# Modulation sums as four 256-column quarters on TensorE's column groups, and the state-space set-up spread over the weight units, in a two-layer hybrid encoder

## Chip, cores and metric

The kernel runs on one core of one Trainium2 chip. The metric is the device time of one execution in microseconds; several executions are timed and their median counts. The profile shows one execution, with its own time.

## What is computed

Two layers of a streaming encoder over 256 tokens of 1024 values, in fp32. Each layer is a SwiGLU feed-forward, a mixer of three heads (sparse attention, a state-space model, a convolution), and a second feed-forward. Each of the three is conditioned by a vector `c`: nine modulation rows of 1024 values per layer, `cond @ mod_w`, give shift, scale and gate.

```python
cond = silu(c)
for l in range(2):
    mod = cond @ mod_w[l] + mod_b[l]          # mod_w[l]: 1024 x 9216
    sh1, sc1, g1, sh2, sc2, g2, sh3, sc3, g3 = split(mod, 9)
    h = rms_norm(x, ffn1_norm[l]) * (1 + sc1) + sh1
    x = x + 0.5 * g1 * swiglu_ffn(h, ffn1_w_gu[l], ffn1_w_down[l])
    h = rms_norm(x, mix_norm[l]) * (1 + sc2) + sh2
    x = x + g2 * hybrid_mixer(h, ...)         # attention | state space | convolution
    h = rms_norm(x, ffn2_norm[l]) * (1 + sc3) + sh3
    x = x + 0.5 * g3 * swiglu_ffn(h, ffn2_w_gu[l], ffn2_w_down[l])
out = rms_norm(x, final_norm)
```

The state-space head needs matrices made from its parameters alone: powers of a complex step, and from them `W`, `O`, `R`, `Ec`, `Es` and `Tp`. The kernel calls this the set-up (`ssm_small`, `ssm_layer`). It doesn't depend on `x`, and must be done before the layer's mixer.

## The kernel before

**The weight stream.** All weights come as units of 128 x 1024 fp32 (`raw`, 512 KB, six buffers), loaded on SP's queue. A weight unit is split in two rounded parts, `hi` on ScalarE (line 100) and `lo` on VectorE (line 102), six buffers each, and each product is three matmuls (lines 328 to 330: hi by high part, lo by high part, hi by low part). A feed-forward works through 11 tiles of 256 hidden columns: four units of gate and up weights (`gt`, results `ps_gt`), then SiLU on ScalarE and the product `h` on VectorE (line 742), split as `hTh` and `hTl`, and then two units of down weights (`ps_y`) of the tile before. The two `ps_gt` banks are free for the next tile only when `h` has been made. In layer 0 the first three tiles run in `start` as `ps_gs`, together with the first modulation columns; their `h` is transposed (`ps_hT`).

**The modulation stream.** Between the weight units stand units of `mod_w` (plan: six of the nine rows in each first feed-forward, two or three in the second one of layer 0, one in the last). VectorE multiplies each by `cond` and adds it to a sum `macc` of 128 x 512 (line 365, two instructions per unit, eight for each half row; two sum buffers). When both halves of a row are there, `mod_flush` adds them over the partitions on TensorE (two fp32 matmuls with `ones`, line 389, to `ps_mod`), copies the result out on ScalarE (`mrow`, line 391), and writes it to DRAM with two transfers on POOL's queue (`spill`, line 394), from where it comes back as columns (`mcol`) or as a row for all partitions.

**The set-up** is a generator that yields after each small step. `stages` is called once for each weight unit (a tick) and takes steps from it: `SLOTS0` for layer 0 in its first feed-forward and `SLOTS1` for layer 1 in the second feed-forward of layer 0, each as first tick, number of ticks, steps per tick. In `start`, `SSTART` steps follow each of eight weight columns.

**The order.** A scheduler writes each engine's list of instructions from the program, its priorities and its own idea of durations. Each engine runs its list in order.

Of the kernel before, what the change touches and what calls it, by code (L numbers as in the profile page):

```python
# [13 lines left out]
AF = mybir.ActivationFunctionType  # L14
# [3 lines left out]
P = 128  # L18
# [8 lines left out]
ADG = (((0,),(1,),(2,3)),((0,1,2,3),))  # L27
HIP = 150
HIPT = 50
SLOTS0 = (4, 40, 2)  # L30
SSTART = 4
SLOTS1 = (2, 60, 2)
UW = 264
NEG_INADM = -3.0e38
NEG_TAKEN = -3.3e38
# [96 lines left out]
def kernel(  # L132
# [8 lines left out]
    nc = tc.nc  # L141
# [22 lines left out]
    def s2(shape, nm, tg="a", dtype=F32):  # L164
        return two_p.tile(shape, dtype, tag="s2" + tg, name=nm, bufs=S2B[tg])
# [15 lines left out]
    ones = const.tile([P, 32], F32, name="ones")  # L181
# [201 lines left out]
    def mod_flush():  # L383
        while len(finished) >= 2:
            l, m, _, acc0 = finished.pop(0)
            acc1 = finished.pop(0)[3]
            ps = bank(ps_m, "ps_mod")
            for h, acc in enumerate((acc0, acc1)):
                nc.tensor.matmul(ps[32 * h:32 * h + 32, :], ones, acc, start=True, stop=True, tile_position=(0, 32 * h))  # L389
            r = s2([64, 512], "mrow")  # L390
            nc.scalar.activation(r, ps[0:64, :], AF.Copy, scale=0.5 if m in (2, 8) else 1.0)  # L391
            d = spill[(l, m)] = tc.dram_tile([1, D], F32, name=f"spill{l}_{m}")
            for h in range(2):
                nc.gpsimd.dma_start(d[:, 512 * h:512 * h + 512], r[32 * h:32 * h + 1, :])  # L394
            if m % 3 != 2:
                nc.gpsimd.dma_start(mc(l, m), d[0].rearrange("(k p) -> p k", p=P))
            if m % 3 == 1:
                nc.gpsimd.tensor_scalar_add(mc(l, m), mc(l, m), 1.0)
                n0 = 8 * (L * (m // 3) + l)
                nc.gpsimd.tensor_mul(mc(l, m), mc(l, m), ncol[:, n0:n0 + 8])  # L400
# [418 lines left out]
    NL = G  # L819
    ssm = {}  # L820

    def ssm_small(l):
        e = nc.vector

        def cp(o, i, scale=1.0):
            nc.scalar.activation(o, i, AF.Copy, scale=scale)
# [3 lines left out]
        def B(nm, shape):  # L830
            n = math.prod(shape)
            if not pool8 or pool8[-1][1] + n > 2048:
                pool8.append([b8([P, 2048], "sp_tmp"), 0])
            t_, o_ = pool8[-1]
            pool8[-1][1] += n
            v_ = t_[:, o_:o_ + n]
            return v_ if len(shape) == 1 else v_.rearrange("p (d n) -> p d n", d=shape[0])
# [92 lines left out]
        yield  # L930

        PQr, PQi = B("pqr", [8, NL]), B("pqi", [8, NL])
        u8, v8 = B("u8", [8, NL]), B("v8", [8, NL])
        qrb = qr.rearrange("p (o n) -> p o n", o=1).to_broadcast([P, 8, NL])
        qib = qi.rearrange("p (o n) -> p o n", o=1).to_broadcast([P, 8, NL])
        cmul(PQr, PQi, PWr[:, 0:8, :], PWi[:, 0:8, :], qrb, qib, u8, v8)
        yield

        cA, cB = T("cA", [8, NL]), T("cB", [8, NL])
        lo_, hi_ = slice(0, 64), slice(64, 128)  # L940
        for tau in range(8):
            d_ = 7 - tau
            cp(cA[lo_, tau, :], PQr[lo_, d_, :])
            cp(cA[hi_, tau, :], PQi[hi_, d_, :])
            cp(cB[lo_, tau, :], PQi[lo_, d_, :], -1.0)
            cp(cB[hi_, tau, :], PQr[hi_, d_, :])
            if tau % 2:
                yield
        oA, oB = T("oA", [8, NL]), T("oB", [8, NL])
        cp(oA[lo_], PWr[lo_, 1:9, :])  # L950
        cp(oA[hi_], PWi[hi_, 1:9, :], -1.0)
# [538 lines left out]
        for g_ in gens:  # L1490
            yield from g_

    def stages(gen, first, n, per):

        def hook(u):
            if first <= u < first + n:
                for _ in range(per):
                    next(gen, None)
            elif u >= first + n:
                for _ in gen:  # L1500
                    pass
        return hook
# [74 lines left out]
```

## Time and profile before

| | |
|---|---|
| median of 3 runs | 1168.14 us (1165.55 to 1171.28) |
| the profiled execution, its own time | 1179.52 us |
| its span | 1177.7 us |
| TensorE busy | 1104.6 us, 94% of the span |
| VectorE busy | 880.2 us, 75% |
| ScalarE busy | 574.4 us, 49% |
| POOL busy | 78.3 us, 7% |
| mean granted clock of TensorE | 0.947 of full |

Busy time is that in which an engine worked on something; where it is near 100%, the engine's own work is the time. A matmul's record is longer than its share of the engine, since matmuls follow each other in a pipeline, so their price is read from one start to the next. The start lasts to about 88 us, the first feed-forward of layer 0 to about 262 us, its mixer to 405 us, its second feed-forward to 630 us; the first feed-forward of layer 1 ends at about 826 us, its mixer at 962 us.

### The profile page before, as it was taken

The page shows a single profiled execution, that of the slowest core. Times are in us where ns is not written, and L with a number is a line of the kernel's source. Part 1 is how long each engine was busy: PE and PEld are TensorE (multiplying, and loading weights), DVE is VectorE, ACT ScalarE, POOL GpSimd, SP SyncE. Part 2 cuts the span into 40 slices and gives each one's busy share as a digit, 9 for nine tenths or more (in the row PEclk, how much of TensorE's full clock was granted, in tenths as well). Part 3 has the DMA queues.
Part 4 walks back from the last instruction along what each step waited for, and adds up shares of the span by engine and source line. Part 5 has one row for each costly group of instructions (what it writes and reads, how often), then busy time and mean ns, then how long its engine had stood idle before and what let it go on. Part 6 is the DMA issues. An engine that isn't in the chain of part 4 may idle for free.

```text
span 1177.7 us, 19146 instructions
## 1 busy us (share of the span) xinstructions
PE 1104.6 (94%) x6979; PEld 944.4 (80%) x6979; DVE 880.2 (75%) x1763; ACT 574.4 (49%) x1035; POOL 78.3 (7%) x144
## 2 busy tenths in 40 slices
PE   5959999998989999889998999999899998999996
PEld 3549888877876779788986888888698687999986
DVE  4779888887667888887757888887667677665655
ACT  4484434346427565744445444443553656544442
POOL 5000021000021000001000000100000000000000
PEclk9979989999798999989999999999989699999999
DMA  9957999995452268678773999989355224767651
GB/s 249 295 182 248 310 312 319 325 282 148 122 118 87 90 197 293 207 229 259 226 223 93 331 337 347 321 300 291 101 157 128 90 89 136 246 209 217 212 162 54
DMA packets 181647, 251.44 MB, mean 214 GB/s; under 512 B 18998, under 2 KB 131840, under 8 KB 181552
## 3 DMA queue, kind: packets, MB, share of 16 engines
q1 hardware_dynamic: 173728, 240.56, 63.7%
q0 software_dynamic: 4768, 7.52, 2.9%
q10 hardware_dynamic: 3056, 2.13, 0.8%
q8 instruction: 55, 0.90, 0.3%
q14 instruction: 40, 0.33, 0.1%
HBM read 245.19 MB, written 1.11 MB: 209 GB/s over the span
## 4 chain that ended last, share of the span: by engine, by line
PE 78%; DVE 9%; DMA 7%; ACT 4%; issue 2%; POOL 0%; ACTq 0%; DVEq 0%; SPq 0%; POOLq 0%
PE ps_gt L328 11%; PE ps_gt L330 11%; PE ps_gt L329 11%; PE ps_y L329 7%; PE ps_y L330 7%; PE ps_y L328 7%; DMA raw<-in_mod_w_dram 3%; DVE lo L102 3%; PE ps_mod L389 2%; DMA U<-uT 1%; PE ps_idx L1198 1%; ACT hf L321 1%; PE ps_cv L1404 1%; PE ps_o L1267 1%; PE ps_gu L328 1%
## 5 line engine op out<-in xcount | busy, mean ns | idle before, releaser
L102 DVE TENSOR_TENSOR lo<-raw,hi 128x1024 fp32r<-128x1024 f32 (+1 forms) x314 | 378.6, 1212 | 141.1 <-ACT hi L100 138.4
L100 ACT ACTIVATE hi<-raw 128x1024 fp32r<-128x1024 f32 (+1 forms) x314 | 327.9, 1055 | 298.7 <-PE ps_gt L329 111.8
L328 PE MATMUL ps_gt<-xTh,hi 128*128 128x256 f32 x1120 | 320.6, 288 | 7.1 <-DVE h L742 7.1
L329 PE MATMUL ps_gt<-xTl,hi 128*128 128x256 f32 x1120 | 319.4, 286 | 0.0
L330 PE MATMUL ps_gt<-xTh,lo 128*128 128x256 f32 x1120 | 317.7, 287 | 0.0
L328 PEld LDWEIGHTS ps_gt<-xTh,hi 128*128 128x128 f32 x1120 | 218.0, 195 | 19.3 <-DVE h L742 7.4
L330 PEld LDWEIGHTS ps_gt<-xTh,lo 128*128 128x128 f32 x1120 | 216.9, 195 | 6.7 <-issue 5.9
L329 PEld LDWEIGHTS ps_gt<-xTl,hi 128*128 128x128 f32 x1120 | 218.6, 195 | 1.8 <-issue 0.8
L365 DVE SCALAR_TENSOR_TENSOR macc<-raw,cond,macc 128x512 f32<-128x512 f32 x224 | 166.4, 747 | 26.1 <-DMA raw<-in_mod_w_dram 24.1
L329 PE MATMUL ps_y<-lo,hTh 128*128 128x512 f32 x352 | 139.5, 396 | 0.9 <-DVE lo L102 0.9
L330 PE MATMUL ps_y<-hi,hTl 128*128 128x512 f32 x352 | 138.2, 393 | 1.0 <-DVE hTl L746 1.0
L328 PE MATMUL ps_y<-hi,hTh 128*128 128x512 f32 x352 | 136.9, 394 | 1.3 <-ACT hTh L745 1.2
L329 PEld LDWEIGHTS ps_y<-lo,hTh 128*128 128x128 f32 x352 | 66.8, 190 | 17.3 <-issue 2.5
L330 PEld LDWEIGHTS ps_y<-hi,hTl 128*128 128x128 f32 x352 | 66.8, 190 | 16.1 <-DVE hTl L746 2.1
L328 PEld LDWEIGHTS ps_y<-hi,hTh 128*128 128x128 f32 x352 | 66.6, 189 | 16.1 <-ACT hTh L745 2.6
L394 POOL DMA_DIRECT2D spill<-mrow x32 | 16.1, 508 | 716.1 <-ACT mrow L391 673.1
L740 ACT ACTIVATE silu<-ps_gt 128x256 f32<-128x256 f32 x70 | 25.7, 381 | 57.8 <-PE ps_gt L330 57.6
L742 DVE TENSOR_TENSOR h<-silu,ps_gt 128x256 f32<-128x256 f32 x70 | 28.5, 415 | 23.3 <-ACT silu L740 23.3
L328 PE MATMUL ps_gu<-hi,xTh 128*128 128x512 f32 x96 | 38.5, 402 | 5.9 <-DVE xTh L324 5.9
L330 PE MATMUL ps_gu<-hi,xTl 128*128 128x512 f32 x96 | 38.5, 401 | 3.1 <-DVE xTl L325 3.0
L329 PE MATMUL ps_gu<-lo,xTh 128*128 128x512 f32 x96 | 37.6, 392 | 0.0
L321 ACT ACTIVATE hf<-ps_ada,mcol 128x128 f32<-128x128 f32 x80 | 29.7, 471 | 10.6 <-PE ps_ada L316 8.6
(384 smaller groups left out, 1630.3 us busy)
## 6 DMA issues: line engine op xcount, KB each, us to landing
raw<-in_ffn_w_gu_dram SPq DMA_DIRECT2D x140, 512.0 KB
raw<-in_mod_w_dram SPq DMA_DIRECT2D x128, 512.0 KB
raw<-in_ffn_w_down_dram SPq DMA_DIRECT2D x88, 512.0 KB
raw<-in_ffn_w_gu_dram SPq DMA_DIRECT2D x72, 256.0 KB
raw<-in_w_in_dram SPq DMA_DIRECT2D x20, 512.0 KB
raw<-in_mod_w_dram SPq DMA_DIRECT2D x32, 256.0 KB
raw<-in_w_out_dram SPq DMA_DIRECT2D x16, 512.0 KB
row<-spill POOLq DMA_DIRECT2D x6, 512.0 KB, 3.9
```

The costliest lines, as they stand in the source:

```text
L100: nc.scalar.activation(hi[:, :n], raw[:, :n], AF.Copy)
L102: nc.vector.tensor_sub(lo[:, :n], raw[:, :n], hi[:, :n].bitcast(F32))
L321: hold[t]["hf", h] = nc.scalar.activation(hf[:, k, :], ps[:, P * k:P * k + P], AF.Identity, bias=mc(l, 3 * i)[:, kk:kk + 1], scale=mc(l, 3 ...
L328: return [nc.tensor.matmul(ps, xh, wh, start=start, stop=False), nc.tensor.matmul(ps, xh, wl, start=False, stop=False), nc.tensor.matmul(p ...
L329: nc.tensor.matmul(ps, xh, wl, start=False, stop=False),
L330: nc.tensor.matmul(ps, xl, wh, start=False, stop=stop)]
L365: nc.vector.scalar_tensor_tensor(acc, raw[:, 512 * i:512 * i + 512], cond[:, k:k + 1], prev, op0=ALU.mult, op1=ALU.add)
L389: nc.tensor.matmul(ps[32 * h:32 * h + 32, :], ones, acc, start=True, stop=True, tile_position=(0, 32 * h))
L394: nc.gpsimd.dma_start(d[:, 512 * h:512 * h + 512], r[32 * h:32 * h + 1, :])
L740: nc.scalar.activation(s, ps[i][:, :256], AF.Silu)
L742: nc.vector.tensor_mul(h, s, ps[i][:, 256:])
L1198: nc.tensor.matmul(ps[:, nk * i:nk * i + nk], qiT[32 * b:32 * b + 32, 256 * i + P * t:256 * i + P * t + P], kiT[32 * b:32 * b + 32, :nk], ...
```

## The change

The two sums of 512 columns become four of 256 columns, on all four column groups of TensorE, with an order token that keeps them together; the copy takes 128 x 256 for 64 x 512, and there are four spill transfers for two. The third number of `SLOTS0` and `SLOTS1` now is the number of steps, spread evenly over the ticks; `SSTART` is 2. In the set-up, the eight powers times `q` are made by doubling (three products of 1, 2 and 4 powers) in the order in which `cA` and `cB` need them, so that four copies on ScalarE do for 32. This makes the set-up one step shorter.

```diff
-SLOTS0 = (4, 40, 2)
-SSTART = 4
-SLOTS1 = (2, 60, 2)
+SLOTS0 = (1, 37, 43)
+SSTART = 2
+SLOTS1 = (1, 42, 58)
...
             ps = bank(ps_m, "ps_mod")
-            for h, acc in enumerate((acc0, acc1)):
-                nc.tensor.matmul(ps[32 * h:32 * h + 32, :], ones, acc, start=True, stop=True, tile_position=(0, 32 * h))
-            r = s2([64, 512], "mrow")
-            nc.scalar.activation(r, ps[0:64, :], AF.Copy, scale=0.5 if m in (2, 8) else 1.0)
+
+            for q in (3, 2, 1, 0):
+                mm_ = nc.tensor.matmul(ps[32 * q:32 * q + 32, 0:256], ones, (acc0, acc1)[q // 2][:, 256 * (q % 2):256 * (q % 2) + 256],
+                                       start=True, stop=True, tile_position=(0, 32 * q))
+                tc.stamp_issue_order_token(mm_.ins, f"mod{l}_{m}")
+            r = s2([P, 512], "mrow")
+            nc.scalar.activation(r[:, 0:256], ps[:, 0:256], AF.Copy, scale=0.5 if m in (2, 8) else 1.0)
             d = spill[(l, m)] = tc.dram_tile([1, D], F32, name=f"spill{l}_{m}")
-            for h in range(2):
-                nc.gpsimd.dma_start(d[:, 512 * h:512 * h + 512], r[32 * h:32 * h + 1, :])
+            for q in range(4):
+                nc.gpsimd.dma_start(d[:, 256 * q:256 * q + 256], r[32 * q:32 * q + 1, 0:256])
...
-        cmul(PQr, PQi, PWr[:, 0:8, :], PWi[:, 0:8, :], qrb, qib, u8, v8)
-        yield
+        e.tensor_copy(PQr[:, 7, :], qr)
+        e.tensor_copy(PQi[:, 7, :], qi)
+        for n in (1, 2, 4):
+            s_, d_ = slice(8 - n, 8), slice(8 - 2 * n, 8 - n)
+            cmul(PQr[:, d_, :], PQi[:, d_, :], PQr[:, s_, :], PQi[:, s_, :],
+                 PWr[:, n:n + 1, :].to_broadcast([P, n, NL]), PWi[:, n:n + 1, :].to_broadcast([P, n, NL]),
+                 t1[:, :n, :], t2[:, :n, :])
+            yield
...
-        for tau in range(8):
-            d_ = 7 - tau
-            cp(cA[lo_, tau, :], PQr[lo_, d_, :])
-            cp(cA[hi_, tau, :], PQi[hi_, d_, :])
-            cp(cB[lo_, tau, :], PQi[lo_, d_, :], -1.0)
-            cp(cB[hi_, tau, :], PQr[hi_, d_, :])
-            if tau % 2:
-                yield
+        cp(cA[lo_], PQr[lo_])
+        cp(cA[hi_], PQi[hi_])
+        cp(cB[lo_], PQi[lo_], -1.0)
+        cp(cB[hi_], PQr[hi_])
+        yield
...
-    def stages(gen, first, n, per):
+    def stages(gen, first, n, steps):
...
-                for _ in range(per):
+                i = u - first
+                for _ in range((i + 1) * steps // n - i * steps // n):
                     next(gen, None)
```

**How it moves the instructions.** On TensorE, the first modulation row in the first feed-forward of layer 0, before; its two matmuls stand in two places, the first behind a down unit and the second in the gate tile after it:

```order
L328 MATMUL ps_y_1046<-hi,hTh 128x512
L329 MATMUL ps_y_1046<-lo,hTh 128x512
L330 MATMUL ps_y_1046<-hi,hTl 128x512
L389 MATMUL ps_mod<-macc,ones 32x512
L328 MATMUL ps_gt_1203<-xTh,hi 128x256
...
L330 MATMUL ps_gt_1203<-xTh,lo 128x256
L389 MATMUL ps_mod<-macc,ones 32x512
L328 MATMUL ps_gt_1204<-xTh,hi 128x256
```

The same row after the change, in the gate tile that follows the start's three (line 390 is the new matmul's, line 994 a transpose of the set-up):

```order
L328 MATMUL ps_gt_1152<-xTh,hi 128x256
L329 MATMUL ps_gt_1152<-xTl,hi 128x256
L330 MATMUL ps_gt_1152<-xTh,lo 128x256
L390 MATMUL ps_mod<-macc,ones 32x256 x4
L994 MATMUL ps_cT<-ident,crr 128x128 x4
L328 MATMUL ps_gt_1153<-xTh,hi 128x256
```

The four stand together. The 32 matmuls of all sums stood in 29 places (26 alone and three pairs); the 64 of now stand in 16.

On VectorE, the end of the start, before: the first products of `W` and `O` (lines 1011 and 1013), then `lo` with the sums of `W` (line 1015) between, then the first `h` (line 756):

```order
L1011 TENSOR_TENSOR sl_O<-CRI,sp_oA 128x512 x4
L1031 TENSOR_TENSOR et<-sl_Ec 128x16
L102 TENSOR_TENSOR lo<-raw,hi 128x1024
L1032 TENSOR_TENSOR et<-sl_Es 128x16
L1015 TENSOR_TENSOR W<-W,wtmp 128x512
L102 TENSOR_TENSOR lo<-raw,hi 128x1024
...
L1015 TENSOR_TENSOR W<-W,wtmp 128x512
L102 TENSOR_TENSOR lo<-raw,hi 128x1024 x2
L1033 TENSOR_TENSOR sl_Ec<-et 128x16
L1013 TENSOR_TENSOR wtmp<-CRI,sp_oB 128x512
L756 TENSOR_TENSOR h<-silu,ps_gs_216 128x256
```

The same place after the change (the lines have moved down by 3; `sp_tmp` and `sp_m` are small set-up vectors):

```order
L102 TENSOR_TENSOR lo<-raw,hi 128x1024 x2
L894 TENSOR_TENSOR sp_tmp<-sp_er,sp_ei 128x16
L895 TENSOR_TENSOR sp_tmp<-sp_ei,sp_er 128x16
L914 TENSOR_TENSOR sp_m_671<-sp_m_671 128x16
L922 RECIPROCAL sp_tmp<-sp_tmp 128x16
L925 TENSOR_TENSOR sp_tmp<-sp_tmp 128x16
L102 TENSOR_TENSOR lo<-raw,hi 128x1024 x2
L896 TENSOR_TENSOR sp_tmp<-sp_tmp 128x16
L926 TENSOR_TENSOR sp_tmp<-sp_tmp 128x16
L1044 MEMSET sl_D_2033 128x16
L102 TENSOR_TENSOR lo<-raw,hi 128x1024
L759 TENSOR_TENSOR h<-silu,ps_gs_216 128x256
```

The big products of the set-up are gone from here; small vectors stand in their place.

On VectorE, what stands ahead of the `h` of the second gate tile of layer 0, before:

```order
L102 TENSOR_TENSOR lo<-raw,hi 128x1024
L365 SCALAR_TENSOR_TENSOR macc<-raw,cond,macc 128x512
L1013 TENSOR_TENSOR wtmp<-CRI,sp_oB 128x512
L1033 TENSOR_TENSOR sl_Ec<-et 128x16x15
L365 SCALAR_TENSOR_TENSOR macc<-raw,cond,macc 128x512
L102 TENSOR_TENSOR lo<-raw,hi 128x1024
L365 SCALAR_TENSOR_TENSOR macc<-raw,cond,bias_94 128x512
L1015 TENSOR_TENSOR sl_O<-sl_O,wtmp 128x512
L742 TENSOR_TENSOR h<-silu,ps_gt_1203 128x256
```

After:

```order
L1014 TENSOR_TENSOR W<-bri,sp_cA 128x512 x4
L365 SCALAR_TENSOR_TENSOR macc<-raw,cond,bias_94 128x512
L1016 TENSOR_TENSOR wtmp<-bri,sp_cB 128x512 x3
L102 TENSOR_TENSOR lo<-raw,hi 128x1024
L1045 TENSOR_TENSOR CmDd<-dKm,ident 128x256
L1014 TENSOR_TENSOR sl_O<-CRI,sp_oA 128x512 x4
L1034 TENSOR_TENSOR et<-sl_Ec 128x16
L1035 TENSOR_TENSOR et<-sl_Es 128x16
L365 SCALAR_TENSOR_TENSOR macc<-raw,cond,macc 128x512
L1018 TENSOR_TENSOR W<-W,wtmp 128x512 x3
L102 TENSOR_TENSOR lo<-raw,hi 128x1024
L745 TENSOR_TENSOR h<-silu,ps_gt_1152 128x256
```

Two products stood there, and now it is fourteen.

## Rows read from the trace of the kernel before

**Rows 1.** The page, busy time, share of the span and instructions of each engine.

```profile
PE 1104.6 (94%) x6979; PEld 944.4 (80%) x6979; DVE 880.2 (75%) x1763; ACT 574.4 (49%) x1035; POOL 78.3 (7%) x144
```

**Rows 2.** Busy time by stretch of the span; the first line names the columns.

```profile
core 0: us, PE busy (x) PEld busy (x) DVE busy (x) ACT busy (x) POOL busy (x), PEclk, DMA share, GB/s
...
90.00:262.00 172.00, 170.29 (x1081) 147.36 (x1081) 148.01 (x225) 70.55 (x101) 15.52 (x27) 0.97 0.91 300
...
505.00:602.00 97.00, 97.00 (x651) 90.07 (x651) 75.65 (x125) 42.66 (x65) 8.25 (x14) 0.94 0.78 249
660.00:700.00 40.00, 40.00 (x263) 35.20 (x262) 34.62 (x47) 18.00 (x25) 1.65 (x3) 1.00 0.99 341
660.00:826.00 166.00, 166.00 (x1103) 145.25 (x1102) 137.23 (x179) 71.53 (x97) 12.12 (x19) 1.00 0.96 319
88.00:94.00 6.00, 5.84 (x29) 5.84 (x30) 6.00 (x13) 1.46 (x5) 0.00 (x0) 0.54 0.71 259
504.00:511.00 7.00, 7.00 (x37) 7.00 (x38) 7.00 (x13) 0.68 (x2) 0.00 (x0) 0.57 0.45 142
```

**Rows 3.** TensorE's timeline at a sum: start, us, line, operation.

```profile
119.36 0.39 PE L329 MATMUL ps_y<-lo,hTh 128*128 128x512 f32 x1
119.59 0.39 PE L330 MATMUL ps_y<-hi,hTl 128*128 128x512 f32 x1
119.91 1.04 PE L389 MATMUL ps_mod<-macc,ones 128*32 128x512 f32 x2
120.89 0.39 PE L328 MATMUL ps_gt<-xTh,hi 128*128 128x256 f32 x1
```

**Rows 4.** All sums as a group (busy us, mean ns), and a pair in the timeline.

```profile
L389 PE MATMUL ps_mod<-macc,ones 128*32 128x512 f32 x64 | 30.3, 605 | 0.0
...
602.66 1.05 PE L389 MATMUL ps_mod<-macc,ones 128*32 128x512 f32 x4
```

**Rows 5.** TensorE's timeline at the convolution of layer 0.

```profile
335.83 8.81 PE L1404 MATMUL ps_cv<-U,sl_W 128*32 128x256 f32 x128 [3.56 <-DMA U<-uT]
344.56 0.39 PE L328 MATMUL ps_inQ<-xTh,hi 128*128 128x256 f32 x1
```

**Rows 6.** TensorE's timeline where it waited for VectorE: idle before, and releaser.

```profile
78.95 0.50 PE L329 MATMUL ps_gs<-lo,xTh 128*128 128x512 f32 x1 [4.19 <-DVE lo L102]
...
88.16 0.69 PE L765 MATMUL ps_hT<-ident,h 128*128 128x128 f32 x2 [6.19 <-DVE h L756]
...
503.87 0.58 PE L328 MATMUL ps_gt<-xTh,hi 128*128 128x256 f32 x1 [7.13 <-DVE h L742]
```

**Rows 7.** VectorE's set-up groups, 60 to 88 us; the last from 90 to 262 us.

```profile
L1013 DVE TENSOR_TENSOR wtmp<-bri,sp_cB 128x512 f32<-128x512 f32 x4 | 2.7, 682 | 0.0
L1011 DVE TENSOR_TENSOR W<-bri,sp_cA 128x512 f32<-128x512 f32 x4 | 2.7, 680 | 0.0
L1015 DVE TENSOR_TENSOR W<-W,wtmp 128x512 f32<-128x512 f32 x4 | 2.7, 674 | 0.0
L1011 DVE TENSOR_TENSOR sl_O<-CRI,sp_oA 128x512 f32<-128x512 f32 x4 | 2.5, 678 | 0.0
...
L1036 DVE TENSOR_TENSOR sl_Es<-et 128x16 f32<-128x16 f32 (+4 forms) x5 | 1.3, 256 | 0.0
```

**Rows 8.** VectorE's waits, 90 to 262 us: us in total, times, longest.

```profile
DVE lo L102 <- ACT hi L100: 15.9, 15, 3.7
DVE h L742 <- ACT silu L740: 6.2, 5, 1.9
```

**Rows 9.** Spill issues, ScalarE's small copies (half of them), VectorE's waits for sums.

```profile
L394 POOL DMA_DIRECT2D spill<-mrow x32 | 16.1, 508 | 716.1 <-ACT mrow L391 673.1
...
L826 ACT ACTIVATE sp_cB<-sp_tmp 64x16 f32<-64x16 f32 x16 | 3.4, 214 | 0.2
...
DVE macc L365: 1.1, 2
```

More of the change, by code (lines that the diff above doesn't have):

```diff
@@ L932, in ssm_small @@
         PQr, PQi = B("pqr", [8, NL]), B("pqi", [8, NL])
-        u8, v8 = B("u8", [8, NL]), B("v8", [8, NL])
-        qrb = qr.rearrange("p (o n) -> p o n", o=1).to_broadcast([P, 8, NL])
-        qib = qi.rearrange("p (o n) -> p o n", o=1).to_broadcast([P, 8, NL])
-        cmul(PQr, PQi, PWr[:, 0:8, :], PWi[:, 0:8, :], qrb, qib, u8, v8)
-        yield
+        e.tensor_copy(PQr[:, 7, :], qr)
[6 more added lines that the diff above has]
+            yield
         cA, cB = T("cA", [8, NL]), T("cB", [8, NL])
         lo_, hi_ = slice(0, 64), slice(64, 128)
-        for tau in range(8):
-            d_ = 7 - tau
-            cp(cA[lo_, tau, :], PQr[lo_, d_, :])
-            cp(cA[hi_, tau, :], PQi[hi_, d_, :])
-            cp(cB[lo_, tau, :], PQi[lo_, d_, :], -1.0)
-            cp(cB[hi_, tau, :], PQr[hi_, d_, :])
-            if tau % 2:
-                yield
+        cp(cA[lo_], PQr[lo_])
[3 more added lines that the diff above has]
+        yield
         oA, oB = T("oA", [8, NL]), T("oB", [8, NL])
```

## The prediction

> **What bounds the kernel now.** I read the page first: the profiled execution took 1179.52 us, its span is 1177.7 us, and TensorE is busy 94% of it [rows 1]. So the span is TensorE's own work plus 73 us of gaps, and the questions are which TensorE work goes, which gaps close, and which other engine is next. For that I read busy time by stretch [rows 2]. The reader should see three kinds of stretch. In the first feed-forward of layer 0 (90 to 262 us) TensorE is busy 170.3 of 172 us, but VectorE 148.0 too and the transfers 0.91. In the second feed-forward of layer 0 TensorE has a gap before 505 us and none after, and VectorE is busy 75.7 of 97 us from there. In the first feed-forward of layer 1 (660 to 826 us) TensorE has no gap, VectorE has room (137.2 of 166 us), and the transfer engines are busy 0.96 of the time, 0.99 in its first 40 us. Then I looked at the gaps one by one in the timeline.
>
> **The modulation sums.** There are 16 flushes, each two fp32 matmuls of 512 columns. One alone holds TensorE from where the next down matmul would have started (119.59 + 0.23 = 119.82 us) to 120.89 us, 1.07 us [rows 3]. Two side by side on two column groups hold it no longer: 1.05 us for the four records at 602.66 us [rows 4]. The order shows 26 of the 32 matmuls alone and three pairs, so 29 blocks x 1.06 = 30.7 us, and the 64 records' busy time agrees, 30.3 us [rows 4]. After the change there are 16 blocks of four 256-column matmuls on four groups. The trace has no such block, but the convolution is the same form: 128 records (64 matmuls of 128*32 by 256 columns, fp32, four groups in turn) from 335.83 to 344.56 us [rows 5], 16 blocks at 0.55 us. With 0.09 us for the gap at entry (119.91 against 119.82) a block costs 0.64 us, all 16 cost 10.3 us, and 20.4 us of TensorE's time go. The bounds are that and four quarters one after the other, 4 x 0.53 = 2.1 us (half the columns of 1.06 us), where nothing goes; I take the convolution's price, since it has the same shape, type and groups. The Trainium skill (TensorE: Matmul & The Clock Gate, "Measured speedup vs the span model") gives 2.38 for three column tiles; scaled to four that is 0.67 us by estimate, which would make the saving some 2 us smaller; the convolution's row is better than the page here.
>
> By stage, from the plan of modulation columns: 12 blocks become 6 in each first feed-forward (12 x 1.06 - 6 x 0.64 = 8.9 us each), 4 become 3 in the second one of layer 0 (2.3 us), one becomes one in the last (0.4 us). What each is worth depends on what else is late there.
>
> **The set-up, start and first feed-forward of layer 0.** Now 32 of its 60 steps run in the start, and the products of W and O stand in VectorE's queue ahead of what TensorE waits for: 4.19 us for a lo at 78.95 us, 6.19 us for h at 88.16 us [rows 6]. In the new order none of these products stands before that lo or that h. The first gap should go. Of the second about 3 us go (four W sums and one product of 0.6 us), and about 3 us stay for the six lo that are still ahead of h. So 7.2 us.
>
> The products don't vanish. Between 60 and 88 us VectorE spends 2.7 + 2.7 + 2.7 + 2.5 = 10.6 us on 16 of them [rows 7]; all move into the stretch from 90 us on. The new chain for the eight powers has 20 small instructions for 6, some 14 x 0.25 = 3.5 us (the price of the E-table's small products [rows 7]; an estimate, between 0 and that). VectorE's work in that stretch becomes 148.0 + 14.1 = 162.1 us. TensorE's becomes 172 - 8.9, less what the half clock cost at its start (0.54 of full speed from 88 to 94 us [rows 2], 2.8 us; the clock had fallen over the two gaps), 160.3 us. VectorE is now the longer one, and it doesn't run without waits: in the 24.0 us that it was idle it waited 15.9 us for hi and 6.2 us for silu [rows 8]. If none of that stays, the stretch takes 162.1 us; if all does, 186.1 us. I take 172, as before, 10 us of waits: ScalarE is busy only 70.6 of 172 us there [rows 2], but a clump of 14 products stands ahead of the second gate tile's h (order above), and hi's own transfers run near full. So the whole 8.9 us saved there is given back to VectorE. The term for both stretches is -7.2 us, with ends at -20 and +7.
>
> **Second feed-forward of layer 0.** Two set-up steps at each tick now put the products ahead of h again: 7.13 us of TensorE's time at 503.87 us [rows 6], then 0.57 of full clock from 504 to 511 us [rows 2], 3.0 us. Spread over 42 ticks they come in the stretch where VectorE has 21 us free. But the spread steps stood in a clump in layer 0 too (order above), so I keep 3 us of the gap and half of the clock's cost. With 2.3 us for the sums the term is 4.1 + 1.5 + 2.3 = 7.9 us, ends 1 and 12.4.
>
> **First feed-forward of layer 1.** No set-up runs there, and VectorE has 29 us free. The 8.9 us need the weights sooner: 319 GB/s x 166 us = 53.0 MB in 157.1 us is 337 GB/s, and the trace's 341 GB/s came with the transfer engines 0.99 busy [rows 2]. That leaves 1%, so I keep 6 of 8.9 us. The Trainium skill (DMA: Bandwidth & Descriptors, "Specifications") puts the limit of HBM for one core at about 358 GB/s; by that 53.0 MB need 148 us, all 8.9 us would be kept and the sum below would be 2.9 us larger. The trace shows 341 at most over 40 us, and I go by it.
>
> **What costs nothing.** Each flush issues four spill transfers for two, 32 more at 508 ns [rows 9], 16.3 us on POOL's queue, which is busy 7% of the time; the scale and gate rows behind them land about 1 us later, half a stage before their use, and in the last stage 20 us before the residual. Without that cover it is 1 us per stage. ScalarE loses 32 copies of 0.214 us per layer [rows 9] and gains four; it was not late but once, before W. The eviction of the sums gets narrower.
>
> **Sum.** 7.2 + 0 + 7.9 + 6 + 0.4 = 21.5 us off 1179.5 us, 1158.0 us. The median of the runs stands at 1168.14 / 1179.52 = 0.990 of the profiled execution, so 1147 us.
>
> **Rivals.** (a) VectorE keeps up everywhere and the transfers too: 10.4 us at the start, 9.9 in the stretch at 162.1 us, 12.4, 8.9 and 0.4 make 42 us, 1126 us. For it: VectorE's free time is real in layer 1; against it: layer 0's sum has none. (b) VectorE keeps all its 24 us of waits in layer 0 (+14.1), and the gap at 503 us only moves (2.3 kept): -7.2 + 14.1 - 2.3 - 6 - 0.4 = -1.8 us, 1166 us, no change. For it: in-order queues put small clumps in front of urgent work in both orders. (c) Slower: the four quarters now stand together, and the first two read the second half's sum. TensorE must stop at each block until VectorE has done the last accumulation, and the next modulation's first accumulation waits in VectorE's queue for the block, as there are two sum buffers. Now only 1.1 us in all are lost so [rows 9]. The saving of 21.5 us over 16 blocks is 1.34 us each; beyond that it loses. At 2.5 us, the order of VectorE's waits for hi (15.9 us in 15 [rows 8], the longest 3.7), 40 - 21.5 gives 1198 us, 1186 us in the runs. Against it: the second half's matmul waits for the same accumulation today. (d) The quarters don't overlap: each block costs 2.1 us, the sums' share of the terms falls away (2.3, 6 and 0.4) and some 3 us are added, 15.1 - 3 = about 10 us gained, 1158 us. The convolution's rows speak against it.
>
> **How the numbers follow.** The forecast gets 0.58, (a) 0.13, (b) 0.15, (c) 0.08, (d) 0.06. The forecast's own range is 1134 to 1161 us, with its largest term, layer 0's first stretches, at either end (20 us gained or 7 lost). To leave out no more than 2 in 10 the range goes on to 1128, toward (a), and to 1168, past (b). Half a percent, 5.8 us, is about what a measurement of this kernel can tell, so faster means below 1162.3 us: 0.55 of the forecast, (a), 0.05 of (d) and 0.03 of (b), together 0.76; same 0.16, slower 0.08.
>
> **What would show it.** Sums: 64 matmuls in 16 blocks of about 0.6 us; some 10 us busy as a union. Start: no gap before lo near 75 us, one of about 3 us before the first h. Layer 0: VectorE busy over 93% from there to the mixer, with TensorE waiting for hi, lo or h, some 10 to 20 us in pieces, and the first adaptive norm of the mixer about 7 us earlier. Second feed-forward: the gap at 503 us under 4 us. Layer 1: the stage 6 us shorter, transfers at 0.98 or more. The prediction is wrong if layer 0 has no such waits (then a), if TensorE idles at the blocks themselves (then c), or if the blocks take over 1 us (then d).

## Result, and the profile after

The changed kernel takes **1159.2 us** (median of eight runs, 1154.4 to 1163.9) against 1169.5 us (eight runs of before, 1164.9 to 1175.3). The ratio is **0.990**, 95% interval 0.986 to 0.993. It is faster, and inside the range, but 12 us above the predicted 1147 us.

The page after, in the columns of [rows 1]:

```profile
PE 1083.5 (94%) x7043; PEld 940.6 (82%) x7043; DVE 881.5 (76%) x1791; ACT 559.7 (49%) x979; POOL 92.5 (8%) x176
```

TensorE lost 21 us of busy time and its share stayed at 94%. The windows view of after, cut where the stages begin, in the columns of [rows 2]. The first row ends at the first transpose of h, and each of the next five at the first transpose of an adaptive norm (which opens a mixer, a feed-forward, and so on):

```profile
0.00:75.67 75.67, 57.21 (x261) 37.64 (x262) 43.44 (x141) 39.41 (x62) 17.33 (x37) 0.95 0.94 272
75.67:265.66 189.99, 178.84 (x1152) 159.30 (x1153) 169.15 (x294) 78.22 (x128) 23.21 (x42) 0.94 0.88 287
265.66:405.66 140.00, 132.72 (x873) 108.60 (x872) 100.32 (x288) 75.10 (x170) 12.86 (x24) 0.85 0.42 113
405.66:613.27 207.61, 200.83 (x1334) 181.52 (x1335) 172.00 (x353) 106.69 (x172) 15.98 (x28) 0.99 0.73 234
613.27:815.05 201.78, 196.33 (x1297) 175.28 (x1296) 172.87 (x250) 93.03 (x140) 17.01 (x33) 0.99 0.90 299
815.05:949.24 134.19, 125.89 (x874) 103.60 (x872) 98.68 (x283) 74.74 (x169) 3.54 (x7) 0.91 0.41 115
949.24:1152.60 203.36, 191.68 (x1256) 174.70 (x1256) 125.00 (x185) 92.54 (x139) 2.52 (x5) 0.98 0.56 179
```

The same cut of the trace of before, for its first two stages and its first feed-forward of layer 1:

```profile
0.00:88.16 88.16, 60.06 (x265) 38.42 (x265) 56.48 (x178) 50.87 (x109) 19.45 (x40) 0.91 0.83 242
88.16:271.27 183.11, 181.40 (x1124) 156.64 (x1125) 156.09 (x243) 73.94 (x109) 16.52 (x29) 0.96 0.90 294
...
627.67:836.97 209.30, 204.42 (x1274) 174.95 (x1272) 172.57 (x250) 94.10 (x140) 12.59 (x21) 1.00 0.87 288
```

The start is 12.5 us shorter and the stretch behind it 6.9 us longer. There TensorE has 8.8 us less of sums, but is busy only 2.6 us less, in part because its mean granted clock is 0.94 for 0.96 of full, and it waits 11.2 us (189.99 - 178.84) where it waited 1.7. VectorE has 13.1 us more work (169.15 for 156.09).

A block of sums in TensorE's timeline, in the first feed-forward of layer 1 (it answers to [rows 3]):

```profile
745.37 0.28 PE L330 MATMUL ps_gt<-xTh,lo 128*128 128x256 f32 x1
745.58 0.64 PE L390 MATMUL ps_mod<-macc,ones 128*32 128x256 f32 x8
746.15 0.38 PE L328 MATMUL ps_gt<-xTh,hi 128*128 128x256 f32 x1
```

The gate matmuls before it start every 0.12 us, so without the block the next one would have started at 745.49; it started at 746.15: 0.66 us. The sums by line, and what TensorE waited for just before them:

```profile
L390 PE MATMUL ps_mod<-macc,ones x128: 378/392/404, 112.6 to 1120.4; 128*32 128x256 f32 x128
...
  issue: 1.3, 4
  DVE lo L102: 0.4, 1
  DVE h L745: 0.4, 1
```

The 64 matmuls (two records each) cost TensorE 2.1 us of waits in all. The gaps that answer to [rows 6], the last also the one at 503.87 us there, and two new ones:

```profile
75.67 0.44 PE L768 MATMUL ps_hT<-ident,h 128*128 128x128 f32 x2 [2.97 <-DVE h L759]
...
155.08 0.51 PE L330 MATMUL ps_gt<-xTh,lo 128*128 128x256 f32 x2 [2.14 <-DVE lo L102]
166.56 0.58 PE L328 MATMUL ps_gt<-xTh,hi 128*128 128x256 f32 x1 [1.99 <-ACT hi L100]
...
512.41 0.39 PE L328 MATMUL ps_gt<-xTh,hi 128*128 128x256 f32 x1 [2.87 <-DVE h L745]
```

The gap before lo is gone, 3 us before h stay, the gap of 7.13 us is 2.87. The new ones are in the stretch to which the set-up was moved, and end with lo or hi.

### The profile page after: what moved, and what is told of

It is laid out like the page before. It is cut to its first block, busy times and chain, and to the rows that moved or that the text cites. A ratio compares the mean times of both kernels' runs of the same rounds, so it can differ in the third digit from the quotient of the medians.

```text
span 1152.6 us, 19302 instructions
## 1 busy us (share of the span) xinstructions
PE 1083.5 (94%) x7043; PEld 940.6 (82%) x7043; DVE 881.5 (76%) x1791; ACT 559.7 (49%) x979; POOL 92.5 (8%) x176
## 4 chain that ended last, share of the span: by engine, by line
PE 53%; DMA 8%; DVE 8%; issue 4%; ACT 3%; SPq 0%; ACTq 0%; POOL 0%; DVEq 0%; POOLq 0%
PE ps_gt L328 6%; PE ps_gt L330 6%; PE ps_gt L329 6%; PE ps_y L328 5%; PE ps_y L330 5%; PE ps_y L329 5%; DVE lo L102 3%; DMA raw<-in_mod_w_dram 2%; PE ps_gu L328 2%; PE ps_gu L330 2%; PE ps_gu L329 2%; DMA U<-uT 1%; DVE macc L365 1%; ACT hi L100 1%; PE ps_idx L1201 1%
## 5 line engine op out<-in xcount | busy, mean ns | idle before, releaser
L328 PE MATMUL ps_y<-hi,hTh 128*128 128x512 f32 x352 | 132.9, 394 | 3.6 <-ACT hi L100 2.8
L397 POOL DMA_DIRECT2D spill<-mrow x64 | 31.3, 496 | 631.2 <-ACT mrow L394 630.5
L329 PEld LDWEIGHTS ps_y<-lo,hTh 128*128 128x128 f32 x352 | 67.6, 192 | 14.8 <-DVE lo L102 2.0
```

The source lines that it names most:

```text
L328: return [nc.tensor.matmul(ps, xh, wh, start=start, stop=False), nc.tensor.matmul(ps, xh, wl, start=False, stop=False), nc.tensor.matmul(p ...
L329: nc.tensor.matmul(ps, xh, wl, start=False, stop=False),
L397: nc.gpsimd.dma_start(d[:, 256 * q:256 * q + 256], r[32 * q:32 * q + 1, 0:256])
```

## Experiments

Ratios are to the kernel before on the same chip, with 95% intervals. The stages below are in microseconds, cut as above in each kernel's own trace ("start" to the first transposed h, "ffn1" to the mixer). The traced execution is one of those that the ratio counts, and not always one near their median.

| | start | ffn1, layer 0 | mixer | ffn2 | ffn1, layer 1 | mixer | last | span | ratio |
|---|---|---|---|---|---|---|---|---|---|
| before | 88.2 | 183.1 | 137.7 | 218.7 | 209.3 | 137.7 | 203.0 | 1177.7 | |
| before, again | 91.5 | 181.6 | 132.8 | 215.2 | 210.2 | 142.5 | 203.0 | 1176.8 | 1.000 (0.997 to 1.004) |
| after | 75.7 | 190.0 | 140.0 | 207.6 | 201.8 | 134.2 | 203.4 | 1152.6 | 0.990 (0.986 to 0.993) |
| after, again | 75.8 | 193.5 | 133.8 | 212.4 | 202.3 | 137.8 | 202.6 | 1158.2 | 0.989 (0.985 to 0.993) |
| sums alone | 88.2 | 185.0 | 132.4 | 214.5 | 204.0 | 137.9 | 202.6 | 1164.7 | 0.995 (0.991 to 0.998) |
| set-up alone | 76.6 | 186.0 | 138.5 | 211.1 | 212.7 | 129.5 | 203.8 | 1158.2 | 0.990 (0.987 to 0.994) |
| old places, layer 0 | 87.5 | 183.8 | 139.0 | 210.4 | 201.4 | 134.6 | 202.6 | 1159.3 | 0.989 (0.984 to 0.993) |
| half accumulation | 76.9 | 176.1 | 131.5 | 210.6 | 201.4 | 140.8 | 202.7 | 1139.9 | 0.976 (0.971 to 0.980) |
| half load | 76.6 | 188.9 | 138.4 | 211.0 | 199.8 | 135.6 | 202.6 | 1153.0 | 0.988 (0.985 to 0.992) |
| pinned steps | 75.7 | 200.2 | 131.5 | 209.2 | 201.8 | 136.0 | 203.2 | 1157.5 | 0.992 (0.989 to 0.996) |
| old sums in layer 0 | 77.0 | 186.3 | 139.8 | 210.9 | 201.7 | 135.9 | 203.3 | 1154.9 | 0.982 (0.978 to 0.986) |
| row 7 in the mixer | 76.3 | 176.6 | 143.5 | 213.2 | 199.7 | 137.0 | 202.8 | 1149.1 | 0.983 (0.980 to 0.985) |
| blocks of twelve | 76.7 | 204.2 | 147.2 | 210.0 | 199.9 | 135.5 | 202.5 | 1176.0 | 0.998 (0.995 to 1.001) |
| pairs of quarters | 77.0 | 189.4 | 135.3 | 209.8 | 199.9 | 142.6 | 202.9 | 1156.8 | 0.988 (0.983 to 0.992) |

**The two controls** are the kernels before and after, unchanged. Of before:

> The kernel before, unchanged, as a control. The profiled execution of before took 1179.5 us while the median of its runs is 1169.5 us, and the profiled execution of after (1154.4 us) is the lowest of its eight. If that difference of some 10 us is only how executions scatter, the ratio is 1.000 +- 0.003 and this second profile has a span nearer 1168 us; I expect most of the scatter in the mixers and in the granted clock, and the three gaps of before (4.2, 6.2 and 7.1 us) at the same places within 1 us. If instead the gaps differ by several us from one execution to the next, the terms of the forecast were read off an unlucky execution.

The gaps are there again (5.2, 5.4 and 6.4 us), so the terms were not read off an accident. But this profiled execution, too, stands near the top of what the kernel shows: 1178.5 us, where its twelve runs go from 1161.9 to 1179.1 with median 1171.9. Of after:

> The changed kernel, unchanged, as a control. In the two profiles of before and the one of after the stages outside the mixers add up to 22 to 24 us of gain, but the medians give only 12. If the profiled execution of after was a good one, this profile shows the start, the first feed-forward of layer 0 and the two after it longer than the first did (75.7, 190.0, 207.6 and 201.8 us), by 5 us or more together; if the difference lies in the mixers alone, these four are the same within 1 us each and the mixers (140.0 and 134.2 us) carry the scatter. The ratio is 0.990 +- 0.003 either way.

Both halves of the expectation hold in part: the first feed-forward is 3.5 us longer, the second 4.8, the two others agree within 0.5, and the mixers trade 6.2 against 3.6 us. One execution tells a stage to some 4 us.

**Sums alone, set-up alone.** The one is the kernel before with the new `mod_flush`; the other the kernel after with the old one:

```diff
-            for q in (3, 2, 1, 0):
+            for h, acc in enumerate((acc0, acc1)):
+                nc.tensor.matmul(ps[32 * h:32 * h + 32, :], ones, acc, start=True, stop=True, tile_position=(0, 32 * h))
...
```

> Only the sums are changed (four quarters on four column groups); set-up as before. Theory of the forecast: the gaps of 4.2, 6.2 and 7.1 us stay, the first feed-forward of layer 0 keeps about 6 of its 8.9 us (VectorE has 148 us of work in 163), the second one 2.3, the first one of layer 1 about 7, the last 0.4: some 15 us, a ratio of 0.987. Rival A, the sums alone carry the whole gain: 0.990, and the set-up alone gives 1.000. Rival B, the closed gaps carry it and the sums are given back everywhere: 0.998 or more.

> Only the set-up is changed (spread, doubling, four copies); the sums are the old pairs of 512 columns. Theory of the forecast: 7.2 us at the start, nothing in the first feed-forward of layer 0 (VectorE has 14 us more there and TensorE waits for it), 5.6 us in the second one, nothing in layer 1: some 13 us, a ratio of 0.989. Together with the sums alone that would be 28 us, more than both at once, because the 8.9 us of sums in layer 0 can be kept only while VectorE is the shorter one. Rival A (the set-up only moves its cost): 1.000. Rival B (the whole gain is the set-up's): 0.990 with the sums alone at 0.998 or more.

The sums give 0.5%, less than the forecast's theory and rival A said and more than B, the set-up 1.0%, and both together 1.0 to 1.1%. That the parts don't add is within the noise of the ratios (1.5% with some 0.5% of uncertainty against 1.0 to 1.1%); the stages show it better. In the first feed-forward of layer 1 the sums give 6 us alone (204.0 against 209.8, the mean of the two traces of before) and the set-up none (212.7). In layer 0 to the mixer, the sums give nothing: 273.2 us from the start, where before has 271.3 and 273.1. The stretch of the run with the sums alone:

```profile
88.19:273.21 185.02, 176.26 (x1148) 157.00 (x1149) 156.60 (x243) 72.39 (x109) 21.02 (x39) 0.95 0.90 291
```

TensorE is busy 5 us less than in the first trace of before, and idle 8.8 us instead of 1.7. Before, it was busy for 181.4 of 183.1 us, and yet less work for it made the stretch no shorter: a share near 100% did not make TensorE's own work the time. The set-up alone brings the mixer to 262.7 us, and the sums added to it take it back to 265.7 and 269.3.

**Old places of the set-up in layer 0**, all else as after:

```diff
-SLOTS0 = (1, 37, 43)
-SSTART = 2
+SLOTS0 = (4, 40, 80)
+SSTART = 4
```

> The changed kernel with the old places of the set-up in layer 0 alone (four steps after each column in the start, then two at each tick from the fourth on); layer 1's set-up spread, new sums, new doubling. Theory of the forecast: the 7 us at the start are lost again, but the first feed-forward of layer 0 keeps about 6 of the 8.9 us that its sums save, so the time is that of the changed kernel within 2 us, a ratio of 0.988 to 0.992 to the kernel before. Rival: the spread in layer 0 is worth its 7 to 10 us at the start in full: 0.996 to 0.998. Other rival: it costs more in the stretch than it gives at the start: 0.985 or less.

As the forecast's theory said: the start is longer by 12 us, the stretch shorter by 6 to 10, and the ratio that of the changed kernel.

**What holds that stretch.** Less work for VectorE, and less to transfer:

```diff
-                    for i in range(2):
+                    for i in range(1 if l == 0 and m < 6 else 2):
```

> The changed kernel with the second of the two accumulations of each modulation unit left out in the first feed-forward of layer 0 (48 instructions of 0.75 us, 36 us of VectorE's 169 us there); transfers and TensorE's work as before, so that half of these modulation sums is missing. Theory V, VectorE holds that stretch: from the first transposed h to the mixer it falls from 190 us to 175 us or less, the ratio to 0.977. Rival D, the transfers hold it (52 MB at some 290 GB/s): it stays within 3 us, 0.988.

```diff
-                        nc.vector.scalar_tensor_tensor(acc, raw[:, 512 * i:512 * i + 512], cond[:, k:k + 1], prev,
+                        nc.vector.scalar_tensor_tensor(acc, raw[:, 512 * (i if l or m > 5 else 0):512 * (i if l or m > 5 else 0) + 512], cond[:, k:k + 1], prev,
...
+                    kk = 2 if l or m > 5 else 1
                     nc.sync.dma_start(
-                        raw.rearrange("p (k n) -> p k n", k=2),
-                        mod_w[l, 256 * q:256 * q + 256, c0:c0 + 512].rearrange("(k p) n -> p k n", p=P))
+                        raw.rearrange("p (k n) -> p k n", k=2)[:, 0:kk, :],
+                        mod_w[l, 256 * q:256 * q + 128 * kk, c0:c0 + 512].rearrange("(k p) n -> p k n", p=P))
```

> The changed kernel with only half of each modulation unit loaded in the first feed-forward of layer 0 (256 KB for 512 KB, 12.6 MB less of some 52 MB) and that half used twice, so that VectorE does exactly as much work; half of the modulation weights are replaced by the other half. Theory V, VectorE holds that stretch: it stays at 186 to 190 us, ratio 0.987 to 0.990. Rival D, the transfers hold it: 12.6 MB at 300 GB/s are 42 us of transfers, and the stretch falls to TensorE's own work, 176 us or less, ratio 0.977. If both this and the run with less VectorE work gain, each waits on the other through the six weight buffers.

Both edits reach rows 2 to 5, two thirds of the units meant, since rows 6 and 7 are in that stretch too: 32 units, 24 us of accumulation or 8.4 MB. With that the answer is still one-sided. The stretch of the first and of the second:

```profile
76.86:252.94 176.08, 171.39 (x1152) 155.18 (x1153) 149.04 (x262) 77.44 (x128) 24.08 (x44) 0.96 0.94 310
```

```profile
76.64:265.54 188.90, 174.93 (x1153) 153.81 (x1153) 168.88 (x294) 78.86 (x128) 23.46 (x42) 0.97 0.78 242
```

With 20 us less on VectorE the stretch is 14 to 17 us shorter, while the transfers run at 310 GB/s and 0.94. (The stages behind it are those of the changed kernel within what two executions differ.) With 0.78 of transfers and VectorE's 169 us it is 1 to 5 us shorter, no more than two executions differ. VectorE holds it, with its work and with its waits for hi (it is idle for 20.8 us of the stretch of after); the transfers alone do not.

**Pinned steps.** In the trace of after, VectorE has 14 of the big products of `W` and `O` between 112.8 and 124.3 us, and SP's timeline has only five weight loads of 512 KB in 16 us there:

```profile
109.69 0.97 SPq L374 DMA_DIRECT2D raw<-in_mod_w_dram  x1
112.93 0.37 SPq L429 DMA_DIRECT2D raw<-in_ffn_w_gu_dram  x1
...
118.94 0.38 SPq L374 DMA_DIRECT2D raw<-in_mod_w_dram  x1
122.55 0.37 SPq L429 DMA_DIRECT2D raw<-in_ffn_w_gu_dram  x1
125.49 0.37 SPq L374 DMA_DIRECT2D raw<-in_mod_w_dram  x1
```

Here each set-up step is queued behind the last lo (`los` collects them in the splitting helper):

```diff
...
-                for _ in range((i + 1) * steps // n - i * steps // n):
-                    next(gen, None)
+                with st.behind([st.los[-1]]):
+                    for _ in range((i + 1) * steps // n - i * steps // n):
+                        next(gen, None)
```

> The changed kernel with each set-up step queued behind the lo that was written last when the step is taken, in both layers: the same instructions, but the big products of W and O stand in pieces of at most three between two lo, where seven or eight stood (on VectorE, 112.8 to 125.4 us in layer 0, only five weight loads were issued in those 16 us). Theory, the clumps hold the weight buffers, the transfers starve and TensorE waits for hi and lo 30 to 50 us later: the first feed-forward of layer 0 falls from 190 us to about 181, the second one by about 2 us, the ratio to 0.981. Rival, VectorE's 169 us of work in that stretch hold it however they are ordered: no change within 2 us, 0.990.

My theory of the clumps falls. With at most three products in a row the stretch is longer, 200.2 us, and TensorE still waits for hi (the lines have moved down by one):

```profile
158.93 1.78 PE L329 MATMUL ps_y<-hi,hTh 128*128 128x512 f32 x4 [2.02 <-ACT hi L101]
184.37 1.19 PE L329 MATMUL ps_y<-hi,hTh 128*128 128x512 f32 x4 [2.67 <-ACT hi L101]
220.22 0.39 PE L329 MATMUL ps_gt<-xTh,hi 128*128 128x256 f32 x1 [2.46 <-ACT hi L101]
262.07 0.80 PE L329 MATMUL ps_y<-hi,hTh 128*128 128x512 f32 x1 [5.44 <-ACT hTh L749]
```

The last one, at the stretch's end, is new; the first three are no shorter than those for hi of after (1.99 and 1.47 us). So the clumps are not what makes TensorE wait for hi. The rival's "no change within 2 us" fails too: the stretch is 7 to 10 us longer, and VectorE, with 170.9 us of work, is idle for 29.3.

**Old sums in the first feed-forward of layer 0 alone** (old loop, `mrow` and spills under `if l == 0 and 2 <= m < 8`, quarters elsewhere):

> The changed kernel with the old sums (two matmuls of 512 columns, two spill transfers) in the first feed-forward of layer 0 alone; the four quarters everywhere else. Theory: VectorE holds that stretch, so the 8.9 us that the quarters take from TensorE become waits for hi, lo and h, and after such waits the granted clock falls to half for some us more; with the old sums the clock stays up. In the run with the set-up alone the mixer of layer 0 began at 262.7 us, with both parts at 265.7 and 269.3 us. So this kernel's mixer begins at 263 +- 1.5 us with a granted clock of 0.98 or more in the stretch, all else as in the changed kernel; ratio 0.985. Rival: the 3 to 7 us are scatter, or come from the order of the set-up's products alone: 266 to 269 us, 0.989.

```profile
76.96:263.28 186.32, 178.73 (x1128) 151.91 (x1129) 169.01 (x294) 79.86 (x128) 18.10 (x30) 0.99 0.89 291
```

The mixer begins at 263.3 us with a granted clock of 0.99, as expected, and the ratio is 0.982: faster than the changed kernel, though the intervals just touch (0.986 ends one, 0.985 begins the other). TensorE is busy 178.7 us here and 178.8 us after, with 8.8 us more of sums here: in the changed kernel the lower clock takes back what the quarters save, and the idle time grows from 7.6 to 11.2 us. The traced execution, 1157.0 us, lies above the median of 1151.3, so its span does not show the gain. This version brings the old copy and the two spill transfers back with the old matmuls, and so does not tell these three apart.

**Row 7 in the mixer.** One modulation row of eight units leaves the stretch:

```diff
-PLAN = [[(2, 3, 4, 5, 6, 7), (), (8, 9, 10)], [(2, 3, 4, 5, 6, 7), (), (8, 9, 10, 11)]]
+PLAN = [[(2, 3, 4, 5, 6), (7,), (8, 9, 10)], [(2, 3, 4, 5, 6, 7), (), (8, 9, 10, 11)]]
```

> The changed kernel with one of the six modulation rows of the first feed-forward of layer 0 (row 7) streamed in the mixer of layer 0 instead: eight units, 12 us of VectorE's work and 4 MB of transfers move to a stage where VectorE is busy 100 of 138 us and the transfers 0.43. Theory V (VectorE holds the first feed-forward): it shortens by 5 to 9 us (the run without 36 us of accumulation gained 15), the mixer grows by 0 to 4; ratio 0.984 to 0.986. Rival: the mixer, where TensorE waits for VectorE's small steps, grows by as much: 0.989 to 0.992.

```profile
76.32:252.90 176.58, 170.77 (x1145) 154.11 (x1146) 158.14 (x278) 78.16 (x127) 20.09 (x37) 0.97 0.87 285
```

VectorE loses 11 us of work, the stretch 13 to 17 (5 to 9 were expected), the mixer grows by 4 to 10 us (0 to 4 expected), and the second feed-forward begins at 396.4 us for 405.7 and 403.1, 7 to 9 us earlier. The 4 MB of transfers left together with VectorE's work, so the run does not tell the two apart. The ratio is 0.983, the second version that beats both kernels. The two together were not run.

**Blocks of twelve.** Do TensorE's waits shrink if it only gets work back? Here the quarters are written three times over in each of those six sums:

```diff
-            for q in (3, 2, 1, 0):
+            for q in (3, 2, 1, 0) * (3 if l == 0 and 2 <= m < 8 else 1):
```

> The changed kernel with the four quarters written three times over in each of the six sums of the first feed-forward of layer 0 (12 matmuls for 4, the same values): 12 blocks of 0.57 us more, 6.9 us of work for TensorE alone, in six lumps. Theory: TensorE is not the bound there, so the mixer of layer 0 begins no later than in the changed kernel (265 to 269 us), its waits shrink by about the 6.9 us, and the granted clock may come back; ratio 0.987 to 0.990. Rival: the lumps delay what VectorE waits for, and the time grows by the 6.9 us: 0.995.

```profile
76.70:280.88 204.18, 183.27 (x1249) 157.29 (x1249) 169.52 (x294) 77.92 (x128) 23.18 (x42) 0.96 0.84 267
```

The theory falls: a block takes 0.9 us more (1.43 us to the next start), 5.2 us in all, and the stretch is 11 to 14 us longer, with 20.9 us of idle TensorE. Work given back in such lumps covers nothing. VectorE's work is the same 169.5 us; it waits more:

```profile
DVE lo L102 <- ACT hi L100: 26.6, 24, 3.5
```

where the trace of after has:

```profile
DVE lo L102 <- ACT hi L100: 14.6, 14, 2.7
```

and the one with the old sums:

```profile
DVE lo L102 <- ACT hi L100: 11.8, 12, 2.0
```

**Pairs of quarters** tells the saving from the place: the quarters of those six sums may stand apart.

```diff
+            alone = l == 0 and 2 <= m < 8
-            for q in (3, 2, 1, 0):
+            for q in (0, 1, 2, 3) if alone else (3, 2, 1, 0):
...
-                tc.stamp_issue_order_token(mm_.ins, f"mod{l}_{m}")
+                if not alone:
+                    tc.stamp_issue_order_token(mm_.ins, f"mod{l}_{m}")
```

> The changed kernel with the four quarters of each sum in the first feed-forward of layer 0 left free to stand apart (no order token there, first half row first). They then stand as twelve pairs, at the places of the twelve 512-column matmuls of the run with the old sums there, and VectorE's list of products is nearly that run's too; a pair takes about half the time of such a matmul, so TensorE has some 6 us less to do than in that run. Theory A, the freed work itself turns into waits and half clock in this stretch: the mixer of layer 0 begins at 266 to 269 us as with the four together, ratio 0.989. Theory B, what costs is that the four stand together and the order that the planner makes round such blocks (the run with twelve matmuls per block was 12 us slower, with more waits, not fewer): the mixer begins at 263 us or earlier, ratio 0.980 to 0.983.

```profile
76.99:266.35 189.36, 177.42 (x1152) 154.32 (x1153) 169.48 (x294) 78.42 (x128) 24.03 (x44) 0.97 0.90 287
```

Theory A's numbers: the mixer begins at 266.4 us, ratio 0.988. The pairs stand where the old matmuls stood, VectorE's work is the same, TensorE's sums are some 5 us shorter (12 x 0.64 for 12 x 1.07), and the stage is 3 us longer, with 11.9 us of idle time and a clock of 0.97. One execution's scatter is as large as 3 us; but the four traces with quarters there and the set-up spread as in the change (265.7, 269.3, 266.4, and 265.5 with half the load) all lie behind the two with the old sums (262.7, 263.3). The copy and the four spill transfers are those of the quarters here, so they remain a rival to the freed work.

## Why the prediction was right, and why it was too low

By stages, the means of the two traces after against the two of before, beside the forecast's terms:

| | forecast | measured |
|---|---|---|
| start and ffn1 of layer 0 | -7.2 | -4.7 (267.5 against 272.2) |
| ffn2 of layer 0 | -7.9 | -6.9 (210.0 against 217.0) |
| ffn1 of layer 1 | -6 | -7.7 (202.0 against 209.8) |
| last ffn | -0.4 | 0.0 |
| mixers | 0 | -2.4 |
| sum | -21.5 | -21.8 (spans) |

**The sums.** A block costs 0.66 us, 0.57 of them behind the entry; the convolution gave 0.64 and 0.55 [rows 5]. The estimate by the Trainium skill (TensorE: Matmul & The Clock Gate, "Measured speedup vs the span model") was 0.67 us, and 0.76 with the 0.09 us of entry that the "some 2 us smaller" counts; the trace is nearer to the convolution. Rivals (c) and (d) are out: TensorE waits 2.1 us at all 16 blocks together, and a block takes 0.66 us, not 2.1. (The sum in (d) should read 12.8 - 3, since 15.1 still holds 2.3 us of sums; its 10 us is right.) In layer 1, where VectorE has room, 7.7 of 8.9 us are kept with both parts and 5.8 with the sums alone, against 6; one execution does not tell these apart. Between the stage's ends, at the places that [rows 2] had at 660 us:

```profile
645.60:685.60 40.00, 40.00 (x275) 36.50 (x274) 34.14 (x46) 18.14 (x26) 2.59 (x5) 1.00 0.96 330
645.60:803.10 157.50, 157.50 (x1132) 145.19 (x1131) 138.13 (x179) 70.68 (x97) 15.60 (x30) 1.00 0.98 329
```

The 0.98 over the stage is as forecast, 329 GB/s for 337. The 341 GB/s were not the most over 40 us: the trace of before has 349 from 676.5 to 716.5 us, and that of after 353 from 680 to 720. The 358 GB/s that the Trainium skill states as the limit of HBM for one core (DMA: Bandwidth & Descriptors, "Specifications"), by which all 8.9 us would be kept, are reached over 40 us in neither trace.

**Start.** The 4.19 us are gone and 2.97 of the 6.19 us stay, as forecast, 7.4 us in all. But the time to the first h falls by 12.5 us: smaller idle times give 2.2 us more (TensorE is idle for 18.5 us, before 28.1), and 2.9 us are its work at a higher granted clock (0.91 to 0.95; busy 60.1 to 57.2 us). Of the half clock I had counted only what lay behind 88 us, in the next stretch.

**First feed-forward of layer 0.** This is the step that failed. VectorE's work came as forecast (+13.1 us for +14.1), but its waits did not shrink from 24 to 10 us: cut at the stage's ends, it was idle for 27.0 and 25.6 us before (183.1 - 156.1, 181.6 - 156.0) and for 20.8 and 24.2 us after (190.0 - 169.2, 193.5 - 169.3). So the stretch grew by 7 to 12 us where I had 0. Rival (b), which kept all of the waits, had 14.1 us there and came nearer. Start and stretch together (-4.7 for -7.2) hide it: two errors of opposite sign, and that their sum came near is luck. "VectorE over 93%" was wrong by the same: 89 and 87%. TensorE's waits, 11.2 and 14.8 us in pieces of up to 2.6 us, were forecast.

I had set the price of a saved microsecond there at zero. With the old set-up the runs say the same (the mixer begins at 273.2 us with the sums alone, at 271.3 and 273.1 before). With the spread set-up it looks a little below zero: quarters in place of the old sums, their copies and spill transfers with them, begin the mixer 2 to 7 us later, four traces against two. Partly these are waits, partly granted clock. That the lower clock follows from the waits is not shown. The clock is 0.99 with 7.4 and 7.6 us idle and 0.94 to 0.97 with 11 to 15, but before it is 0.96 with 1.7 us idle, and with half the accumulation 0.96 with 4.7; and some of the half clock comes without a wait (last section). The blocks of twelve show only that not any work of TensorE cures it.

Why VectorE waits longer for hi once TensorE's sums are shorter stays open. The trace of after shows what it hangs on, between 77 and 266 us: hi on ScalarE waits for weights to land, and SP issues loads only when VectorE's lo and sums have freed a buffer.

```profile
ACT hi L100 <- DMA raw<-in_ffn_w_gu_dram: 48.7, 21, 4.4
ACT hi L100 <- DMA raw<-in_ffn_w_down_dram: 26.8, 11, 6.3
...
SPq L374 <- DVE lo L102: 23.6, 17, 2.6
SPq L374 <- DVE macc L365: 16.5, 13, 3.7
```

hi waits 75.5 us for weights there, and 70.3 (50.6 and 19.7) with the old sums. VectorE, buffers, transfers and hi form a ring; which of them gives way first no run shows.

**Second feed-forward of layer 0.** The gap of 7.13 us is 2.9 and 3.9 us, as forecast. The set-up alone gives 5.9 us (217.0 to 211.1), the sums alone 2.5 (217.0 to 214.5).

**From trace to median.** The traces differ by 21.8 us, the medians by 10 to 12. I took the sum off an execution of 1179.5 us and scaled it by 0.990; that moves a difference of 21.5 us by 0.2 us only. Both traced executions of before are near the top of its runs (1179.5 and 1178.5, where the jobs' runs go from 1161 to 1183 with medians of 1169 to 1174); those of after stand on either side of its medians of 1158 and 1159 (1154.4 and 1160.0). On average the traced executions of before lie 8 us above their medians and those of after 1 us below, which is the difference: it seems that part of what the traces of before lost, a typical execution does not lose, so that the agreement of 21.8 with 21.5 us is in part luck. The mixers alone, untouched, took 267.5 to 282.7 us together in the kernels that left them alone and computed everything, at a granted clock of 0.81 to 0.92. Which stage is shorter in an execution of before that takes its median can't be said, since none was traced.

## What to carry to other kernels

Price a saving stage by stage: TensorE's 8.9 us were worth 6 to 8 where the other engines had room, and nothing or a little less where VectorE held the stage, although TensorE was busy 99% of it. There, moving a modulation row away (11 us of VectorE's work and 4 MB of transfers) gave 13 to 17 us in the stage and 7 to 9 to the end of the mixer. When two parts of a change meet in one stage, try each with and without the other: here 0.5% and 1.0% made 1.0%, and leaving one part out of one stage gave 1.8%. And take a difference of sums from an execution near the median, or from two.

## What the runs showed that I had not expected

**Half clock without a wait.** In the trace of after TensorE runs 32 matmuls of 16 columns of the set-up (`ps_K`) in the stretch where VectorE is late. Some 2.5 us after the first of them the granted clock falls to half, and TensorE is busy all that time:

```profile
231.55 4.60 PE L1066 MATMUL ps_K<-CmDd,W 128*128 128x16 f32 x32
...
234.00:240.80 6.80, 6.80 (x28) 5.97 (x28) 6.76 (x11) 2.13 (x3) 4.04 (x7) 0.50 0.97 307
```

That is 3.4 of the some 11 us of full clock that this stretch lost (0.06 of 190 us). In the trace of before the clock falls in the same way at 161.8 us, behind `ps_K` at 159.0 us. With the old sums in layer 0 it stays up:

```profile
217.05 3.64 PE L1077 MATMUL ps_K<-CmDd,W 128*128 128x16 f32 x32
...
217.00:228.00 11.00, 11.00 (x90) 9.88 (x90) 10.00 (x13) 4.06 (x6) 4.21 (x8) 1.00 0.97 323
```

In ten of the fourteen traces the clock falls within 5 us of the start of these matmuls, and in four (set-up alone, old sums in layer 0, pairs, blocks of twelve) it does not; why is open. So the place of this block is one more rival to the quarters for a part of the 2 to 7 us, but not for the pairs.

**Two and four quarters.** That four 256-column fp32 quarters on four column groups hold TensorE for 0.57 us from the block's first start to the next matmul's (745.58 to 746.15) was forecast. Two hold it as long:

```profile
106.33 0.62 PE L391 MATMUL ps_mod<-macc,ones 128*32 128x256 f32 x4
106.89 0.39 PE L328 MATMUL ps_gt<-xTh,hi 128*128 128x256 f32 x1
```

0.56 us, while one 512-column matmul alone takes 0.98:

```profile
106.29 1.05 PE L392 MATMUL ps_mod<-macc,ones 128*32 128x512 f32 x2
107.27 0.39 PE L328 MATMUL ps_gt<-xTh,hi 128*128 128x256 f32 x1
```

In these rows the time goes with the columns of one group, whether two or four groups work.
